# A list job that yields ahead of its TensorE steps, with look-ups asked in pairs and marked one ahead

## Chip, core and metric

The kernel runs on one core of a Trainium2 chip. The metric is the device time of one execution in microseconds, taken as the median of the runs shown.

## What is computed

One decoder layer over 256 tokens of width 2048: an attention part (a differential attention beside a sparse one), a norm, a retrieval part called PEER, and a second norm. The change lies in the retrieval part. Each token picks 8 x 16 of 16,384 experts by product keys, and the layer sums the picked rows of `v`, weighted by a gate and by the gelu of a product with the rows of `u`:

```
top_s, pos = lax.top_k(cand, PEER_TOPK)
eidx = jnp.take_along_axis(cidx, pos, axis=-1)
g = jax.nn.softmax(top_s, axis=-1)
ue = u[eidx]
h = jnp.einsum('cd,chkd->chk', xc, ue).astype(jnp.float32)
a = jax.nn.gelu(h, approximate=False) * g
ve = v[eidx]
return jnp.einsum('chk,chkd->cd', a.astype(ve.dtype), ve)
```

Not every expert is wanted by a token of the 256. So the kernel reads the first 32 groups of 128 experts whole, and of the other groups only the rows that somebody wants: it builds a list of wanted experts and gathers their rows by it. The list job is what the change rewrites.

## The kernel before

All engines run from one program order that is fixed while the program is built. Weight work comes in 273 units (`units`). A unit is 1 MB of weights: it is loaded (`dma_unit`, L165), split into a high part `wh` (ScalarE, ACT) and a low part `wl` (VectorE, DVE), and used in four quarters of matmuls on TensorE (PE). Units 77 to 108 are the whole groups of `u`. Units 109 to 162 (the C units) hold gathered rows of `u`: GpSimd (POOL) issues an indirect DMA from an index column, the rows are turned on PE (`turn_quarter`, L211, the rows `psa<-ident,raw`) one unit ahead, and then used. A quarter of a C unit is so one turn of 4 matmuls and 8 matmuls `psb<-xx`. C units 109 to 115 use tiles of 256 columns, the later ones up to unit 154 of 512. Units 163 to 272 are the value stage: rows of `v`, gathered and used without a turn.

A unit's weights are asked for three units ahead, and six units ahead in the value stage.

Beside the units run jobs, which are Python generators. After each quarter `run_units` (L268) calls `pump` (L235). It steps each job once, in the order in which they were started, up to the next `yield`. With a slack (2.5 us here, `SLACK_GATE`) it stops as soon as the builder's own estimate of the ACT or DVE clock is ahead of that of PE by more than the slack. A job that yields a positive number isn't stepped before that much estimated time is over. Three jobs matter:

- The list job (`job_list`, L1020). It makes a key for every group and position, sorts with 16 rounds of MAX8 and MATCH_REPLACE8 on DVE, finds the beginnings of the parts of the list with four small matmuls (`less`, `ones`, result `tot`) in the first round, turns the sorted keys into differences (`shift`, `edge`, copied into `dx`), and then makes 38 look-ups. One look-up marks on DVE (`sg`, one to three tiles), multiplies on PE (`psa<-dx,sg`, three matmuls for each mark tile), and reads the result on DVE (`at`, three times `lw`) and ACT (`i2l`). After look-ups 4, 9, 12, 17, 22, 28 and 38 `known` turns what was found into index columns (`vidx` for gathers of rows, `aidx` for gates).
- The gate job (`job_gates`, L1001), 32 steps for the second half of the tokens. A step makes one-hot tiles on DVE (two `oh` and one `og`), multiplies the tiles of two steps before on PE (`psa<-og,oh`, 8 matmuls) and copies out on ACT (`stg`). 32 more steps of the first half run earlier, in `job_count`.
- The singles (`job_singles`, L1280): 28 rows that one token alone wants, each with two gathers of 1 MB (`sr`), in four groups that begin with seven small gathers (`gsr`). They start at the unit at which the gate job has ended (`single_from`, L1554) and then follow the units' count, one for 1.5 C units.

Where a unit's gather needs an index column that the list hasn't reached, `column` (L179) pumps without slack until it is there: all jobs are stepped in turns, and no unit's matmul is put between. This comes three times: at unit 106 for the first 12 columns, at unit 118 for columns 27 to 35, and at unit 127 for columns 51 to 65. This text calls these places the first, second and third forced stretch.

## Time and profile before

| | us |
|---|---|
| median of 3 runs | 1737.91 (1737.27 to 1738.87) |
| profiled execution, device time | 1734.11 |
| its span, first to last instruction | 1732.2 |
| PE, share of the span busy | 93% |
| DVE, share of the span busy | 75% |

The profiled execution is 3.8 us (0.2%) below the median. PE is the engine that is nearly always at work, so the question for every stage is when it isn't, and what ended its wait. Note that the ends of matmuls are modelled: a stretch in which PE shows busy throughout may still run below PE's rate. PEclk is the clock granted to PE as a share of full speed; its two levels are 1.0 (2.4 GHz) and 0.5 (1.2 GHz), and a mean between them is a mixture.

### The profile page before, as it was taken

The numbers are of one execution on the slowest core, as the hardware profiler recorded it, in microseconds if no ns is written. First come the engines' busy times: TensorE is split into PE (matmuls) and PEld (weight loads), VectorE is DVE, ScalarE is ACT, GpSimd is POOL, SyncE is SP. The second block draws the span as 40 slices with busy tenths as digits, with TensorE's granted clock in tenths as the row PEclk, the third lists the DMA queues.
The fourth block names the chain that finished last, engine by engine and source line by source line (L and its number), as shares of the span: only waits on it lengthen the run. The fifth ranks groups of instructions, "written<-read, shape, count | busy, mean of one in ns | idle before, by whom it ended". The sixth has DMA issues, their size and how long they took to land.

```text
span 1732.2 us, 25235 instructions
## 1 busy us (share of the span) xinstructions
PE 1606.4 (93%) x9151; PEld 1364.4 (79%) x9151; DVE 1307.0 (75%) x2844; ACT 817.7 (47%) x1370; POOL 596.5 (34%) x558
## 2 busy tenths in 40 slices
PE   7999999998989899959979899999979999999994
PEld 6888888877878788849969788888857777788872
DVE  5686767656999887875976667786678888777767
ACT  5445555445424565323635333344445555555533
POOL 0033100015778400002001033334566666556742
PEclk9999999999989999979979899999999999999998
DMA  7454454545444434926324878798999999998861
GB/s 275 163 178 146 150 190 147 217 178 194 161 147 165 171 110 132 300 68 208 111 74 154 250 287 341 272 392 311 419 351 406 387 389 381 372 331 310 300 255 55
DMA packets 112531, 409.18 MB, mean 236 GB/s; under 512 B 11216, under 2 KB 62608, under 8 KB 69648
## 3 DMA queue, kind: packets, MB, share of 16 engines
q0 software_dynamic: 37856, 246.96, 37.4%
q1 hardware_dynamic: 74400, 160.27, 27.2%
q8 instruction: 74, 1.21, 0.3%
q14 instruction: 57, 0.47, 0.1%
q10 hardware_dynamic: 144, 0.26, 0.0%
HBM read 376.00 MB, written 31.39 MB: 235 GB/s over the span
## 4 chain that ended last, share of the span: by engine, by line
PE 64%; DVE 20%; DMA 6%; issue 4%; ACT 3%; POOL 2%; SPq 0%; DVEq 0%; ACTq 0%; POOLq 0%
PE psa L116 34%; PE psb L116 31%; DVE wl L116 6%; DVE oh L116 2%; ACT wh L116 2%; POOL gsr L187 1%; DMA gr<-gtab,aidx 1%; DMA sr<-x1d,xidx 1%; DVE lw L116 1%; DMA raw<-in_v_dram,vidx 1%; DVE tv L116 1%; DVE ti L116 1%; DVE yacc L116 1%; DVE eid L116 1%; DVE og L116 1%
## 5 line engine op out<-in xcount | busy, mean ns | idle before, releaser
L116 PE MATMUL psb<-xx,wh 128*128 128x512 f32 (+1 forms) x1407 | 504.8, 393 | 0.0
L116 DVE TENSOR_TENSOR wl<-raw,wh 128x1024 fp32r<-128x1024 f32 (+2 forms) x278 | 321.6, 1172 | 101.8 <-ACT wh L116 101.5
L116 PE MATMUL psb<-xx,wl 128*128 128x256 f32 x1392 | 373.6, 283 | 5.2 <-DVE wl L116 3.9
L116 ACT CAST wh<-raw 128x1024 fp32r<-128x1024 f32 (+1 forms) x278 | 283.5, 1044 | 65.4 <-PE psa L116 26.8
L116 PE MATMUL psa<-xx,wh 128*128 128x512 f32 x800 | 291.1, 407 | 9.4 <-DVE xx L116 8.3
L116 PEld LDWEIGHTS psb<-xx,wh 128*128 128x128 f32 x1407 | 268.3, 192 | 36.1
L116 PEld LDWEIGHTS psb<-xx,wl 128*128 128x128 f32 x1392 | 266.8, 192 | 11.3 <-DVE wl L116 5.4
L187 POOL DMA_INDIRECT raw<-in_un_dram,vidx x54 | 54.7, 1014 | 480.3 <-PE psa L116 252.1
L116 PE MATMUL psa<-xx,wl 128*128 128x256 f32 x800 | 219.2, 284 | 0.9 <-DVE wl L116 0.8
L116 DVE TENSOR_TENSOR wl<-psa,wh 128x512 fp32r<-128x512 f32 x216 | 146.6, 686 | 75.2 <-ACT wh L116 74.7
L116 ACT CAST wh<-psa 128x512 fp32r<-128x512 f32 x216 | 126.6, 587 | 149.9 <-PE psa L116 147.8
L116 PEld LDWEIGHTS psa<-xx,wh 128*128 128x128 f32 x800 | 151.0, 192 | 42.9 <-ACT wh L116 10.0
L116 PEld LDWEIGHTS psa<-xx,wl 128*128 128x128 f32 x800 | 153.9, 192 | 6.6 <-DVE wl L116 2.1
L116 DVE TENSOR_TENSOR wl<-rawv,wh 128x1024 fp32r<-128x1024 f32 x106 | 125.7, 1222 | 28.3 <-ACT wh L116 25.7
L116 PE MATMUL psa<-ident,raw 128*128 128x128 f32 x864 | 130.7, 274 | 3.4 <-DMA raw<-in_un_dram,vidx 3.4
L116 ACT CAST ah<-ar 128x256 fp32r<-128x256 f32 (+1 forms) x82 | 30.3, 370 | 201.3 <-DVE ar L116 192.3
L116 PE MATMUL psb<-wl,ah 128*128 128x512 f32 x276 | 110.2, 399 | 7.2 <-DVE wl L116 7.2
L116 PE MATMUL psb<-wh,ah 128*128 128x512 f32 x276 | 110.3, 400 | 3.4 <-DVE bl L116 2.6
L116 PEld LDWEIGHTS psa<-ident,raw 128*128 128x128 f32 x864 | 103.7, 142 | 11.8 <-issue 3.7
L116 PE MATMUL psa<-wh,ah 128*128 128x512 f32 x268 | 106.7, 398 | 4.9 <-ACT wh L116 4.9
L116 PE MATMUL psa<-wl,ah 128*128 128x512 f32 x268 | 107.7, 402 | 3.0 <-DVE wl L116 2.6
L116 PE MATMUL psb<-wh,al 128*128 128x512 f32 x276 | 109.1, 395 | 0.0
(305 smaller groups left out, 3050.7 us busy)
## 6 DMA issues: line engine op xcount, KB each, us to landing
raw<-in_win_dram SPq DMA_DIRECT2D x42, 1024.0 KB, 4.9
raw<-in_ut_dram SPq DMA_DIRECT2D x32, 1024.0 KB, 5.1
raw<-in_wo_dram SPq DMA_DIRECT2D x18, 1024.0 KB, 4.9
raw<-in_wq_dram SPq DMA_DIRECT2D x16, 1024.0 KB, 4.9
gtab<-stg SPq DMA_DIRECT2D x32, 512.0 KB, 5.4
cdr<-bl SPq DMA_DIRECT2D x39, 128.0 KB, 4.6
ar<-cdr SPq DMA_DIRECT2D x39, 128.0 KB, 7.1
hd<-bl SPq DMA_DIRECT2D x32, 128.0 KB, 1.7
```

Source lines behind the costliest of these rows:

```text
L116: return f(*a, **k)
L187: nc.gpsimd.indirect_dma_start(dst, None, src, bass.IndirectOffsetOnAxis(ap=index, axis=0))
```

## The change

Five edits, all in the list job:

- It yields before the four small matmuls for `tot`, and before the `shift` and `edge` matmuls.
- `begin` is one TENSOR_TENSOR of 304 elements in place of eight TENSOR_SCALAR of 38.
- ACT copies the first half of `dx` and DVE the second; before, ACT copied both large halves, and DVE the four small pieces.
- The first four look-ups are asked in pairs: marks of three look-ups first, then the matmuls of two look-ups, the fourth's marks, the matmuls of the next two, and the reads behind each pair's yield.
- From the fifth on, a look-up's marks are made right behind the read of the one before, and a look-up has two yields (the second asks for 2 us) in place of three.

```
@@ job_list
                 DVE.tensor_copy(t16, t8)
+                yield
                 ps = psA()
                 PE.matmul(ps[:, 0:8], less, c16, start=True, stop=False)
...
-                for c in range(8):
-                    DVE.tensor_scalar(begin[:, c], first, tot[:, c:c + 1], None, op0=OP.add)
+                DVE.tensor_tensor(begin, first[:, None].to_broadcast([P, 8, A]),
+                                  tot[:, 0:8, None].to_broadcast([P, 8, A]), op=OP.add)
...
         ACT.copy(XY[:, 0:P], srt)
+        yield
...
-        for h in range(2):
+        for h, copy in enumerate((ACT.copy, DVE.tensor_copy)):
             c, o = slice(4 * h, 4 * h + 4), h * m
-            ACT.copy(dx[:, c, 0:P], ps[:, None, o:o + P].to_broadcast([P, 4, P]))
...
+            copy(dx[:, c, 0:P], ps[:, None, o:o + P].to_broadcast([P, 4, P]))
...
-        for a, (part, q) in enumerate(ASK):
...
-                sg[c] = ls.tile([P, 3 * P], F16, name="sg", tag="sg", bufs=3)
-                DVE.tensor_scalar(sg[c], places, begin[:, c, a:a + 1], None, op0=OP.is_ge)
-            if a >= 4:
-                yield
...
+        def mark(a):
+            part, q = ASK[a]
+            marks[a] = {c: ls.tile([P, 3 * P], F16, name="sg", tag="sg", bufs=4)
+                        for c, at in start_of[part] if 3 * q + 2 >= at}
+            for c, sg in marks[a].items():
+                DVE.tensor_scalar(sg, places, begin[:, c, a:a + 1], None, op0=OP.is_ge)
...
+        for a in range(3):
+            mark(a)
+        yield
+        for a in (0, 2):
+            find(a)
+            find(a + 1)
+            if a == 0:
+                mark(3)
+            yield
+            read(a)
+            read(a + 1)
+        known(0, CUTS[0])
+        asked = CUTS[0]
+        mark(4)
+        yield 2000.0
+        for a in range(4, A):
+            find(a)
+            yield
+            read(a)
+            if a + 1 < A:
+                mark(a + 1)
             if 3 * (a + 1) in CUTS:
                 known(asked, 3 * (a + 1))
                 asked = 3 * (a + 1)
-            yield
+            yield 2000.0
```

`find(a)` holds the matmuls of look-up a, `read(a)` its `at`, `i2l` and `lw`.

Where the instructions come to stand follows from the jobs' turns. Three places:

DVE in the first forced stretch, from the copies into `dx` on. Before:

```order
L116 CAST dx<-psa 128x4 x4
L116 TENSOR_SCALAR sg<-places,begin 128x384
L116 SCALAR_TENSOR_TENSOR at<-psa,mine 128x3
L116 SCALAR_TENSOR_TENSOR lw,keys<-row,at,psa 128x128 x3
L116 TENSOR_SCALAR sg<-places,begin 128x384
```

After:

```order
L116 CAST dx<-psa 128x4x128
L116 CAST dx<-psa 128x4 x2
L116 TENSOR_SCALAR sg<-places,begin 128x384 x6
L116 SCALAR_TENSOR_TENSOR at<-psa,mine 128x3
L116 SCALAR_TENSOR_TENSOR lw,keys<-row,at,psa 128x128 x3
```

All six mark tiles of the first four look-ups stand ahead of the first read, where each look-up's marks stood behind the read of the one before. On PE the 18 matmuls of the four look-ups follow one another in both kernels, and then the same 64 matmuls of units 106 to 108 up to the first turn; the 8 matmuls of a quarter that stood between the `tot` and the `shift` matmuls now stand ahead of the `tot` matmuls.

DVE in the second forced stretch, from one look-up's read to the next one's (`oh`, `oh`, `og` are a gate step). Before:

```order
L116 SCALAR_TENSOR_TENSOR lw,keys<-row,at,psa 128x128 x3
L116 TENSOR_TENSOR oh_8700<-iota_3638,iT 128x512
L116 TENSOR_TENSOR oh_8701<-iotab,iT 128x512
L116 TENSOR_TENSOR og<-oh_8701,gpc 128x1024
L116 TENSOR_SCALAR sg<-places,begin 128x384 x2
L116 TENSOR_TENSOR oh_8720<-iota_3638,iT 128x512
L116 TENSOR_TENSOR oh_8721<-iotab,iT 128x512
L116 TENSOR_TENSOR og<-oh_8721,gpc 128x1024
L116 TENSOR_TENSOR oh_8743<-iota_3638,iT 128x512
L116 TENSOR_TENSOR oh_8744<-iotab,iT 128x512
L116 TENSOR_TENSOR og<-oh_8744,gpc 128x1024
L116 SCALAR_TENSOR_TENSOR at<-psa,mine 128x3
```

After:

```order
L116 SCALAR_TENSOR_TENSOR lw,keys<-row,at,psa 128x128 x3
L116 TENSOR_SCALAR sg<-places,begin 128x384 x2
L116 TENSOR_TENSOR oh_8617<-iota_3638,iT 128x512
L116 TENSOR_TENSOR oh_8618<-iotab,iT 128x512
L116 TENSOR_TENSOR og<-oh_8618,gpc 128x1024
L116 TENSOR_TENSOR oh_8640<-iota_3638,iT 128x512
L116 TENSOR_TENSOR oh_8641<-iotab,iT 128x512
L116 TENSOR_TENSOR og<-oh_8641,gpc 128x1024
L116 SCALAR_TENSOR_TENSOR at<-psa,mine 128x3
```

Two gate steps for a look-up in place of three, and the marks ahead of both. From the first turn to the end of the second forced stretch PE has 25 sets of 8 gate matmuls before and 18 after (with the same 40 quarters); from there to the end of the third 7 and 14 (with the same 36 quarters). In the third forced stretch PE has 30 look-up matmuls in a row before and 18 after; the other 12 stand in two quarters ahead of it.

POOL's queue at the passage into the value stage. Before, ahead of and behind the fourth group's seven small gathers:

```order
L187 DMA rawv<-in_v_dram,vidx 128x2048
L187 DMA gsr<-gtab,gi 128x128 x7
L187 DMA gr<-gtab,aidx 128x256
L187 DMA raw<-in_v_dram,vidx 128x2048
L187 DMA gr<-gtab,aidx 128x256
```

After, at the same place (a single's two gathers):

```order
L187 DMA raw<-in_v_dram,vidx 128x2048
L187 DMA sr<-in_un_dram,vidx 128x2048
L187 DMA sr<-x1d,xidx 128x2048
L187 DMA gr<-gtab,aidx 128x256
L187 DMA rawv<-in_v_dram,vidx 128x2048
```

The gate job ends four units later, so `single_from` is 135 in place of 131. 19 singles stand ahead of the first gather from `v` before, 16 after; the fourth group's seven gathers stand 15 issues of POOL behind that first gather from `v` before, 54 behind it after (rows of the same gather counted once), and the last single is done at unit 239 in place of 217.

## Rows read from the trace of the kernel before

**Rows 1.** The page: busy time of each engine, and the granted clock of PE in 40 equal slices of the span.

```profile
PE 1606.4 (93%) x9151; PEld 1364.4 (79%) x9151; DVE 1307.0 (75%) x2844; ACT 817.7 (47%) x1370; POOL 596.5 (34%) x558
...
PEclk9999999999989999979979899999999999999998
```

**Rows 2.** Busy time by stretches, cut at the places that the list touches. The columns: the stretch, its length, then busy us (and instructions) of PE, PEld, DVE, ACT and POOL, PEclk, the share of the DMA engines busy, GB/s.

```profile
748.60:789.60 41.00, 20.12 (x101) 16.39 (x101) 27.41 (x140) 6.02 (x15) 3.75 (x3) 0.71 0.17 55
...
816.50:868.40 51.90, 50.34 (x404) 47.57 (x403) 46.90 (x111) 30.25 (x51) 5.09 (x5) 1.00 0.34 117
868.40:890.80 22.40, 11.90 (x90) 9.61 (x90) 20.24 (x63) 8.56 (x12) 0.00 (x0) 0.58 0.00 1
890.80:966.00 75.20, 74.92 (x505) 67.55 (x504) 48.99 (x133) 37.01 (x69) 8.58 (x9) 0.99 0.56 187
966.00:978.50 12.50, 5.08 (x35) 3.56 (x36) 7.47 (x41) 0.81 (x5) 0.00 (x0) 0.71 1.03 279
978.50:1120.00 141.50, 136.26 (x923) 120.36 (x921) 97.81 (x267) 54.22 (x122) 45.30 (x48) 0.99 0.77 283
1120.00:1256.00 136.00, 129.03 (x925) 119.03 (x923) 99.69 (x198) 58.82 (x130) 57.78 (x57) 1.00 0.95 372
1256.00:1300.00 44.00, 34.88 (x134) 25.70 (x133) 31.56 (x45) 19.29 (x26) 29.98 (x27) 0.92 0.91 352
1300.00:1500.00 200.00, 198.59 (x846) 157.92 (x845) 164.03 (x210) 111.14 (x145) 129.64 (x106) 1.00 0.98 386
1500.00:1690.00 190.00, 187.04 (x800) 149.68 (x799) 140.41 (x190) 101.64 (x125) 111.18 (x102) 1.00 0.84 306
```

**Rows 3.** Who kept PE waiting from 740 to 1300 us: total us, times, longest us.

```profile
PE psa L116 <- DVE sg L116: 28.9, 15, 4.1
PE psa L116 <- DVE XX L116: 9.1, 1, 9.1
...
PE psa L116 <- DVE c L116: 4.1, 1, 4.1
```

**Rows 4.** PE's timeline in the first forced stretch: start, length, engine, line, operation, tiles, shapes, count, and in brackets the idle time before it and what ended it.

```profile
752.71 0.17 PE L116 MATMUL psa<-c,less 128*128 128x8 f16 x1 [4.13 <-DVE c L116]
...
764.91 1.25 PE L116 MATMUL psa<-XX,shift 128*128 128x137 f32 x4 [9.07 <-DVE XX L116]
...
768.68 0.51 PE L116 MATMUL psa<-dx,sg 128*128 128x130 f16 x3 [2.06 <-DVE sg L116]
...
777.00 0.78 PE L116 MATMUL psb<-xx,wh 128*128 128x512 f32 x1
```

**Rows 5.** Timelines of DVE, ACT and POOL in the same stretch, in order of time; the last row is a VectorE operation on 512 elements read from PSUM, from a later place.

```profile
753.82 1.28 DVE L116 TENSOR_SCALAR begin<-first,tot 128x38 f32<-128x38 f32 x8
...
764.47 0.29 DVE L116 MAX8 XX<-key 128x8 f32<-128x128 f32 x1
...
766.65 0.58 ACT L116 CAST dx<-psa 128x512 f16<-128x512 f32 x1 [1.56 <-PE psa L116]
...
769.22 0.16 DVE L116 SCALAR_TENSOR_TENSOR at<-psa,mine 128x3 f32<-128x3 f32 x1 [0.60 <-PE psa L116]
...
770.74 0.32 DVE L116 TENSOR_SCALAR sg<-places,begin 128x384 f16<-128x384 f16 x1
...
779.88 0.17 DVE L116 CAST vidx<-keys 128x12 int32<-128x12 f32 x1
...
781.07 1.20 POOL L187 DMA_INDIRECT raw<-in_un_dram,vidx  x1 [194.37 <-DMA hd<-bl]
...
845.11 0.69 DVE L116 TENSOR_TENSOR wl<-psa,wh 128x512 fp32r<-128x512 f32 x1 [0.75 <-ACT wh L116]
```

**Rows 6.** The view of DMA issues: a gather of C rows, how many, median us from issue to landing.

```profile
raw<-in_un_dram,vidx POOLq DMA_INDIRECT x54, 6.0
```

**Rows 7.** DVE's timeline in the second forced stretch: one gate step, one read, the next gate step, the marks.

```profile
875.46 0.68 DVE L116 TENSOR_TENSOR oh<-iota,iT 128x512 f16<-128x512 f16 x1
...
877.19 0.15 DVE L116 SCALAR_TENSOR_TENSOR at<-psa,mine 128x3 f32<-128x3 f32 x1
...
878.68 0.69 DVE L116 TENSOR_TENSOR oh<-iota,iT 128x512 f16<-128x512 f16 x1
...
880.41 0.54 DVE L116 TENSOR_SCALAR sg<-places,begin 128x384 f16<-128x384 f16 x2
```

**Rows 8.** PE's timeline: a set of gate matmuls and what follows it at full clock; the first look-up of the second forced stretch and the turn that ends the stretch; a look-up of the third forced stretch and the turn that ends it.

```profile
855.67 1.09 PE L116 MATMUL psa<-og,oh 128*128 128x128 f16 x8
856.51 0.48 PE L116 MATMUL psb<-xx,wh 128*128 128x512 f32 x1
...
873.64 0.95 PE L116 MATMUL psa<-dx,sg 128*128 128x130 f16 x6 [4.11 <-DVE sg L116]
...
890.81 1.04 PE L116 MATMUL psa<-ident,raw 128*128 128x128 f32 x4
...
968.54 0.69 PE L116 MATMUL psa<-dx,sg 128*128 128x130 f16 x6 [1.85 <-DVE sg L116]
...
977.44 1.06 PE L116 MATMUL psa<-ident,raw 128*128 128x128 f32 x4
```

**Rows 9.** POOL's timeline at the fourth group's small gathers, first and last of seven.

```profile
1271.56 1.68 POOL L187 DMA_INDIRECT gsr<-gtab,gi  x1 [4.07 <-DVE gi L116]
...
1279.95 0.94 POOL L187 DMA_INDIRECT gsr<-gtab,gi  x1 [0.31 <-issue]
```

More of the change, by code (lines that the diff above doesn't have):

```diff
@@ L1133, in job_list @@
         yield
-        for h in range(2):
+        for h, copy in enumerate((ACT.copy, DVE.tensor_copy)):
             c, o = slice(4 * h, 4 * h + 4), h * m
-            ACT.copy(dx[:, c, 0:P], ps[:, None, o:o + P].to_broadcast([P, 4, P]))
-            DVE.tensor_copy(dx[:, c, P:P + 1], ps[:, o + P + 4 * h:o + P + 4 * h + 4, None])
-            DVE.tensor_copy(dx[:, c, P + 1:P + 2], ps[:, None, o + P + 8:o + P + 9].to_broadcast([P, 4, 1]))
+            copy(dx[:, c, 0:P], ps[:, None, o:o + P].to_broadcast([P, 4, P]))
+            copy(dx[:, c, P:P + 1], ps[:, o + P + 4 * h:o + P + 4 * h + 4, None])
+            copy(dx[:, c, P + 1:P + 2], ps[:, None, o + P + 8:o + P + 9].to_broadcast([P, 4, 1]))
         keys, i2l = F([P, A, 3], "keys"), ls.tile([P, A, 3], F32, name="i2l", tag="XY")
@@ L1162, in known, with find, read @@
             keep["known"] = b
-        asked, start_of = 0, {"S0": ((0, 0),), "S1": ((1, 0),), "C": ((2, 0), (4, LC1), (5, LCS)),
-                              "D": ((3, 0), (6, LD1), (7, LDS))}
-        for a, (part, q) in enumerate(ASK):
-            cs = [c for c, at in start_of[part] if 3 * q + 2 >= at]
-            sg = {}
-            for c in cs:
-                sg[c] = ls.tile([P, 3 * P], F16, name="sg", tag="sg", bufs=3)
-                DVE.tensor_scalar(sg[c], places, begin[:, c, a:a + 1], None, op0=OP.is_ge)
-            if a >= 4:
-                yield
-            ps = psA()
+        start_of = {"S0": ((0, 0),), "S1": ((1, 0),), "C": ((2, 0), (4, LC1), (5, LCS)),
+                    "D": ((3, 0), (6, LD1), (7, LDS))}
+        marks, found = {}, {}
+        def mark(a):
[4 more added lines that the diff above has]
+                DVE.tensor_scalar(sg, places, begin[:, c, a:a + 1], None, op0=OP.is_ge)
+        def find(a):
+            ps, sgs = psA(), marks.pop(a)
+            cs = list(sgs)
             for j in range(3):
                 for c in cs:
-                    PE.matmul(ps[:, j * n:(j + 1) * n], sg[c][:, j * P:(j + 1) * P], dx[:, c],
+                    PE.matmul(ps[:, j * n:(j + 1) * n], sgs[c][:, j * P:(j + 1) * P], dx[:, c],
                               start=(c == cs[0]), stop=(c == cs[-1]))
-            pj = ps[:, 0:3 * n].rearrange("p (j x) -> p j x", j=3)
-            yield
+            found[a] = ps[:, 0:3 * n].rearrange("p (j x) -> p j x", j=3)
+        def read(a):
+            pj = found.pop(a)
             at = ls.tile([P, 3], F32, name="at", tag="at", bufs=2)
@@ L1190, in job_list @@
                 asked = 3 * (a + 1)
-            yield
+            yield 2000.0
         fl = F([P, 11], "fl")
```

## The prediction

> **What bounds the kernel now.** I read the page first: PE is busy 93% of the span, DVE 75%, and in the middle third of the slices the granted clock falls below full [rows 1]. So I looked for the stretches in which PE isn't fed, and cut the span there [rows 2]. From 748.6 to 789.6 us PE works 20 of 41 us; from 868.4 to 890.8 it works 12 of 22.4, at a mean clock of 0.58; from 966.0 to 978.5 it works 5 of 12.5. These are the three forced stretches. Two more are less plain: from 816.5 to 868.4 PE shows 50.3 of 51.9 us, but DVE too shows 46.9, so DVE nearly sets the pace there; and the passage into the value stage, 1256 to 1300, leaves PE idle for 9.1 us. The waits name the cause: 28.9 us in 15 waits for marks (`sg`), 9.1 for the end of the sort (`XX`), 4.1 for the first counts (`c`) [rows 3]. DVE works in order, so a wait for marks is a wait for everything that stands ahead of them on DVE: reads, and in the second forced stretch gate steps.
>
> From 1300 us on PE is busy 198.6 of 200 and 187.0 of 190 us [rows 2]. What is won before stays won, unless transfers are late.
>
> **First forced stretch.** The yields do not remove it: unit 106 still asks for columns that the list hasn't, so all jobs are pumped with no unit between. What moves is one quarter. Before, its 8 matmuls came after the `tot` matmuls; now they run ahead of them, at full clock and in time in which PE waited 4.13 us for `c` [rows 4]. The sort that ends with MAX8 at 764.76 [rows 5] holds PE in either kernel, so this moves no end. `begin` does: eight operations took 1.28 us from 753.82, on the chain of the sort. One of 304 elements lies between the 0.16 us of a tiny operation and the 0.69 of 512 elements [rows 5]; I take 0.5, so the sort ends 0.7 sooner, at 764.05. `shift` and `edge` follow as before, and the copies into `dx`, which began at 766.65, can begin at 765.95.
>
> Before, ACT's half took 0.58 and its second half waited for DVE's small pieces, so that the first look-up began at 768.68 [rows 4, 5]. Now both halves begin at 765.95. DVE's takes about 0.69 (its row of 512 elements from PSUM), two small copies 0.25, the first mark 0.3: the first look-up begins near 767.3, 1.4 sooner. The four look-ups are 18 matmuls. Three take 0.51 [rows 4], at the low clock, so 18 take 2.9; marks cost DVE 0.23 each behind the first and keep up. PE is through at 770.1. Before, each look-up also waited for the read of the one before (1.5 us from `at` at 769.22 to the next mark at 770.74 [rows 5]), and PE went on at 777.00 [rows 4]. That is 6.9 sooner. Of the 64 matmuls that follow (11 us in either kernel) the first came at half clock before; a little less of them will now, so the first turn could begin near 781.5 in place of 789.6.
>
> But the turn needs the first gather, and that needs the reads. They are still serial on DVE: six marks end near 768.6, four reads of 1.5 end at 774.7. Before, 3.05 us lay between 777.00 and the end of `vidx` at 780.05, of which 0.3 were the wait for the last matmuls and 1.5 the last read: 1.25 for `known`'s way to `vidx`, which so comes at 775.9. POOL issues 1.0 later as before, and the gather lands 6.0 after that [rows 5, 6]: 782.9. So PE waits about 1.3 us for it, a wait that wasn't there. **Gain 6.7 us** (41.0 becomes 34.3). Bounds: 4 if the gather takes 2.7 us more than the median, 8 if it doesn't hold PE.
>
> **Up to the second forced stretch** the list needs two turns of the jobs for a look-up instead of three, and fewer gate steps stand there: of 25 sets of gate matmuls up to the end of the second forced stretch 18 are left. 12 in place of 16 fall between 816.5 and 868.4. A gate step takes DVE 1.73 us (877.19 - 875.46 [rows 7]), so DVE loses 6.9 us; but one read (1.49), one mark and a `known` (about 1.6 with the operations behind `vidx`) come in from the forced stretch, net 3.6 less. PE loses four sets of 0.84 [rows 8], 3.4. With both engines near full, and gate steps now in some quarters only, I take **a gain of 2 us**; bounds 0 and 4.
>
> **Second forced stretch.** Between two look-ups DVE had two gate steps, a read, a gate step and the marks, 7.15 us for each (873.64 to 880.79 by PE). Now: a read and the marks, 1.95 us, then two gate steps, 3.46; and the first look-up's marks are made before the stretch. By DVE's order: gate, gate, read, marks (5.4), the same again (5.4), and the third look-up starts 10.8 us in; its six matmuls, 0.7 to 0.9, and two sets of gate matmuls, 1.7 at full clock, 2.2 taken, then the turn: 13.6 us against 22.4. **Gain 8.8 us**; bounds 5.2 (only the three gate steps fewer) and 10.5. A part of this, the 3.1 us of read and `known` counted above, is paid there.
>
> **Up to the third forced stretch** the gate steps come back: 14 sets in place of 7 in the same 36 quarters. PE is the bound here (74.9 of 75.2 us, DVE 49.0 [rows 2]), so each costs its matmuls, 0.84 us: 5.9 us. Two look-ups that were in the third forced stretch stand here too, 12 matmuls, 0.7 us at full clock. DVE has 26 us free and gets 12.1 + 3.5 of them filled; where a gate step and a read fall into one quarter it has 0.7 + 1.7 + 1.7 to do against PE's 1.9 + 0.84 (75.2 us less seven sets, by 36 quarters), and sets the pace there, for which I add 1.4. **Loss 8 us**; bounds 6.6 and 13 (seven steps at DVE's 1.73, and the finds).
>
> **Third forced stretch.** A look-up's marks still follow the read of the one before, so a run of look-ups still waits 1.85 us in each [rows 8]. But there are three in place of five: two times 1.85 + 0.69 less, so that the 11.4 us from the stretch's start at 966.0 to the turn at 977.44 [rows 2, 8] become 6.3. With the low clock behind it (0.71 in the stretch's row) in part kept off, **gain 6 us**; bounds 4 and 7.
>
> **Later look-ups.** Between 978.5 and 1120 PE is idle for 5.2 us [rows 2], most of it for marks. With marks made a turn ahead I take **a gain of 3**; bounds 0 and 5, since DVE also stands behind the singles' small gathers there, which nothing removes.
>
> **Passage into the value stage.** From 1120 to 1300 PE is idle 7.0 + 9.1 = 16.1 us [rows 2]. In the passage POOL waits 4.07 us and issues seven small gathers from 1271.56 to 1280.9 [rows 9]: for 14 us no row of `v` is asked for, with three units asked ahead. That group now comes some 40 issues later, where six units are asked ahead, and this stall should go; but three singles more, 6.3 MB, fall into a stage in which the DMA engines are 0.91 to 0.98 busy at 386 GB/s [rows 2], and the third group comes nearer to the passage. 6.3 MB are 16 us of transfer at that rate if nothing hides them. I take **a gain of 2** and bounds of 9 gained and 8 lost.
>
> **Sum:** 6.7 + 2 + 8.8 - 8 + 6 + 3 + 2 = 20.5 us off the profiled execution's 1734.1, 1713.6; that execution is 3.8 below the median, so in terms of the median 1737.9 - 20.5 = **1717.4**.
>
> **Rivals.**
> - *The gate steps come back at DVE's price.* If DVE and not the list sets the pace from 816 to 966, moving steps wins little: nothing ahead of the second forced stretch, 5.2 in it, a loss of 10 after it, 6.7 and 4 in the other two, 1 later, 1 in the passage. 7.9 us, 1730. For it: DVE's 46.9 of 51.9. Against: DVE's 49.0 of 75.2 where the steps go [rows 2].
> - *The passage loses its stall.* With the fourth group out of it and nothing given back: 9 in place of 2, and 1 or 2 more in the earlier terms, 29 us, 1709.
> - *Transfers bind the value stage.* Then the 6.3 MB cost 16 us, and the fourth group's block of 14 us on POOL costs its whole length, since in a stage bound by transfers every us without a request is lost; singles at the same pace up to unit 239 leave no slack to make it good. Of the gain 20.5 - 2 are left, minus 30: 1749, slower. It decides if the share of busy DMA stays near 1 until the last single. For it: 0.98 from 1300 to 1500. Against: 0.84 from 1500 on, 30 us of free transfer time, and PE's 198.6 of 200 [rows 2]. The Trainium skill, "DMA: Bandwidth & Descriptors", section "Where 436 GB/s comes from", says that a core's transfers between HBM and SBUF are held to about 358 GB/s; by that rule this rival would be the forecast. The trace does not agree: it moves 386 GB/s for 200 us.
> - *The change does nothing*, since every wait is in forced stretches and these remain: each term at its low bound, 3 + 0 + 5.2 - 13 + 4 + 0 + 0, about zero: 1738.
>
> **How the numbers follow.** The forecast 0.58, its own span 1712 to 1724; the first rival 0.18, the second 0.13, the third 0.06, the last 0.05. A measurement of this kernel can tell about 0.2%, 3.5 us, from no change. Faster: 0.58 + 0.18 + 0.13 = 0.89; within 0.2%: 0.05; slower: 0.06. The range leaves out the last two and the far ends of the others: 1705 to 1732.
>
> **What would show it.** In the changed profile: a look-up run of 18 matmuls without waits near 767 us; one wait of PE for a gather, 1 to 2 us, near 782; a second forced stretch of 13 to 15 us; the stretch from its end to the next forced one longer by 7 to 9, with DVE near 64 us busy; no wait above 1 us for marks after that. Wrong would be: waits for `og` in place of those for `sg`, or waits for `raw` or `rawv` gathers behind 1300.

## The result

| | us |
|---|---|
| before, median of 5 runs | 1738.87 (1737.27 to 1742.22) |
| changed, median of 5 runs | 1726.66 (1724.44 to 1729.97) |
| ratio, 95% interval | 0.9925 (0.9908 to 0.9943) |
| profiled execution of the changed kernel; its span | 1727.36; 1725.2 |

The change makes the kernel faster by 0.75%, 12 to 13 us. The forecast was 1717.4, with 1705 to 1732 as the range: the range held, the forecast's own span (1712 to 1724) missed by 2.7, and of the 20.5 us forecast some 12 came.

**The profile after, by stretches.** The first view is busy time cut where [rows 2] were cut, at the corresponding places, in the same columns:

```profile
751.30:784.50 33.20, 16.98 (x93) 14.70 (x92) 25.87 (x129) 5.00 (x15) 3.93 (x3) 0.69 0.13 45
...
860.60:873.50 12.90, 6.80 (x53) 5.51 (x53) 11.64 (x34) 3.95 (x6) 0.00 (x0) 0.60 0.00 0
873.50:956.60 83.10, 83.07 (x579) 75.62 (x577) 62.87 (x172) 44.07 (x78) 9.07 (x9) 0.98 0.47 158
956.60:961.80 5.20, 1.53 (x12) 1.01 (x13) 3.37 (x18) 0.32 (x2) 0.00 (x0) 0.71 0.92 247
961.80:1103.70 141.90, 139.03 (x965) 125.02 (x963) 98.88 (x299) 54.25 (x127) 38.52 (x39) 0.99 0.79 285
...
1232.00:1280.00 48.00, 39.52 (x164) 31.53 (x165) 33.69 (x45) 23.46 (x34) 27.16 (x24) 0.93 0.92 365
1280.00:1480.00 200.00, 194.27 (x809) 152.72 (x808) 160.43 (x208) 105.94 (x136) 128.83 (x110) 0.98 0.96 377
```

The first forced stretch has gone from 41.0 to 33.2 us (1.4 of that is the quarter that now stands ahead of it), the second from 22.4 to 12.9, the third from 12.5 to 5.2, and the stretch between the second and the third has grown from 75.2 to 83.1, with PE busy throughout: the gate steps are there now. The last row is the surprise. PE did 846 matmuls in the first 200 us behind the passage [rows 2]; now it does 809, with 5.7 us idle.

Who kept PE waiting from 740 to 1300 us (us, times, longest), to be held against [rows 3]:

```profile
PE psa L116 <- DVE sg L116: 11.2, 6, 2.4
PE psa L116 <- DVE XX L116: 11.0, 1, 11.0
...
PE psa L116 <- DVE c L116: 2.7, 1, 2.7
```

28.9 us of waits for marks became 11.2, and 15 waits became 6. The wait for the sort grew by 1.9 us and the one for `c` shrank by 1.4: the quarter that was moved ahead of the `tot` matmuls no longer fills the wait behind them.

**Where the time went, aligned.** Executions differ in their first 730 us too, where the programs are the same. So for each kernel the table takes the start of the same PE matmul in its trace, less that in the trace of the kernel before, less the same difference at a matmul that starts at 730.46 us before (1.3 us for the changed kernel, -0.6 to 3.3 for the others). The row names are its start in the kernel before. Negative is sooner. The columns behind "after" are the experiments below, by their numbers.

```
   before  after    e1    e2    e3    e4    e5    e6    e7    e8    e9   e10   e11   e12
   789.58   -6.4   0.2  -5.2  -6.3  -6.2  -0.5  -6.3  -5.4  -6.2  -5.6  -6.3  -5.5  -5.6  first turn
   864.03   -9.0  -0.3  -7.9  -8.9  -8.8  -3.1  -7.3  -8.7  -8.8  -7.3  -8.9  -8.7  -7.3  last turn ahead of stretch 2
   890.81  -18.6   0.1 -17.4 -18.5 -18.4 -12.7  -5.3 -25.6 -18.4 -24.3 -18.5 -25.8 -24.1  turn that ends stretch 2
   963.78  -10.8   0.7 -10.3 -10.8 -11.2  -5.5  -6.7 -11.1 -10.6  -9.8 -11.3 -11.1  -9.7  last turn ahead of stretch 3
   977.44  -16.9   1.0 -16.4 -16.9 -17.4 -11.6  -3.6 -20.6 -16.8 -19.3 -17.5 -20.6 -19.2  turn that ends stretch 3
  1117.19  -18.1   3.0 -15.7 -16.7 -18.5 -13.1  -9.9 -23.1 -17.0 -21.7 -19.3 -23.7 -21.9  behind the look-ups
  1221.23  -21.4   4.4 -20.5 -13.5 -21.9 -17.9  -8.9 -25.5 -18.5 -21.4 -21.4 -30.7 -28.8  ahead of the passage
  1303.93  -18.5   5.0 -17.2 -12.6 -18.5 -15.3  -4.7 -17.7 -18.4 -18.6 -29.8 -36.6 -29.3  value stage, first use of ah + 96
  1407.40   -8.9   5.0  -8.0  -4.8 -16.5  -6.2  -0.8 -16.4 -14.1 -14.8 -28.0 -32.9 -25.5  first use of ah + 352
  1708.15   -8.1   4.8  -6.1  -5.1 -14.6  -6.1  -1.8 -13.0 -14.6 -14.9 -21.5 -28.0 -21.2  first use of ah + 1080
```

Up to 1304 us the changed kernel is 18.5 us ahead. By 1407 it is 8.9 ahead: **9.6 us are lost in the value stage**, where the prediction had nothing. The loss shows again in the columns of e2 (9.2) and e5 (9.1), which have the fourth group at the same place, and not in that of e1, which has it where it was. (The profiled execution of before, 1734.11, is 4.8 below the median of its 5 runs, that of e1 3.6 above its own. So the end of a column says less than the medians; a column against its neighbours, stretch by stretch, says more. The last row is one of the last matmuls; what follows it is not in the table.)

**The place of the loss.** POOL's timeline of the changed kernel:

```profile
1330.40 1.93 POOL L187 DMA_INDIRECT rawv<-in_v_dram,vidx  x1 [1.98 <-DVE one L116]
1336.47 1.68 POOL L187 DMA_INDIRECT gsr<-gtab,gi  x1 [4.14 <-DVE gi L116]
...
1345.31 0.95 POOL L187 DMA_INDIRECT gsr<-gtab,gi  x1 [0.30 <-DMA gsr<-gtab,gi]
1346.56 1.02 POOL L187 DMA_INDIRECT raw<-in_v_dram,vidx  x1 [0.30 <-issue]
1347.88 0.94 POOL L187 DMA_INDIRECT gr<-gtab,aidx  x1 [0.30 <-issue]
```

The fourth group's seven small gathers first wait 4.14 us for their index `gi`, then take ten, and from 1332.3 to 1346.6 no row of `v` and no row of gates is asked for. DVE and PE behind that, each from its own timeline:

```profile
1352.90 0.43 DVE L116 TENSOR_TENSOR ar<-ar,gr 128x256 f32<-128x256 f32 x1 [4.95 <-DMA gr<-gtab,aidx]
```

```profile
1354.77 0.80 PE L116 MATMUL psa<-wh,ah 128*128 128x512 f32 x1 [2.36 <-ACT ah L116]
```

The gate row asked for at 1347.88 is the one that DVE waits for, and `ah` is made from it. The stretches around it, in ten-microsecond pieces:

```profile
1340.00:1350.00 10.00, 10.00 (x45) 8.04 (x44) 6.96 (x9) 4.40 (x5) 7.87 (x8) 1.00 0.36 101
1350.00:1360.00 10.00, 7.18 (x21) 5.05 (x20) 5.97 (x9) 4.39 (x5) 7.09 (x7) 0.74 1.01 393
1360.00:1370.00 10.00, 9.89 (x40) 7.64 (x39) 7.97 (x11) 4.50 (x6) 6.83 (x6) 0.92 0.93 345
1370.00:1380.00 10.00, 8.95 (x37) 6.44 (x36) 9.00 (x11) 4.40 (x5) 6.72 (x5) 1.00 1.01 410
```

The DMA engines fall to a busy share of 0.36, and then PE starves: 21, 40 and 37 matmuls in pieces that hold 44 at full pace, 34 too few, which at 10/44 us each are 7.7 of the 9.6 us. Only 4 us of that are idle time (30 less the three busy times); the rest is PE at a granted clock of 0.74 and 0.92 behind the wait.

**The passage itself** is hardly better. With the fourth group gone from it, PE still idles 8.5 of the 48 us from 1232 to 1280, where it idled 9.1 of 44 before. Its longest wait is 3.97 us, up to 1268.22, and the longest piece of the chain of waits up to it (start, length, what) is this:

```profile
1252.97 13.36 DMA gr<-gtab,aidx
```

A row of gates took 13.4 us from issue to landing there, with no small gather near it.

### The profile page after: what moved, and what is told of

Same layout as the page of the kernel before. It is cut to its first block, busy times and chain, and to the rows that moved or that the text cites. A ratio compares the mean times of both kernels' runs of the same rounds, so it can differ in the third digit from the quotient of the medians.

```text
span 1725.2 us, 25232 instructions
## 1 busy us (share of the span) xinstructions
PE 1609.9 (93%) x9151; PEld 1371.0 (79%) x9151; DVE 1304.4 (76%) x2836; ACT 815.2 (47%) x1371; POOL 598.2 (35%) x558
## 4 chain that ended last, share of the span: by engine, by line
PE 65%; DVE 18%; DMA 5%; issue 5%; ACT 3%; POOL 3%; SPq 0%; DVEq 0%; ACTq 0%; POOLq 0%
PE psa L116 33%; PE psb L116 32%; DVE wl L116 6%; ACT wh L116 2%; DVE oh L116 2%; DMA gr<-gtab,aidx 2%; POOL gsr L187 1%; DMA raw<-in_win_dram 1%; DVE tv L116 1%; DVE ti L116 1%; DVE yacc L116 1%; DVE eid L116 1%; DVE lw L116 1%; DMA rawv<-in_v_dram,vidx 1%; DVE cand L116 1%
## 5 line engine op out<-in xcount | busy, mean ns | idle before, releaser
L187 POOL DMA_INDIRECT gr<-gtab,aidx x82 | 96.2, 1174 | 40.5 <-issue 22.2
```

The lines of the kernel that those rows point to most:

```text
L187: nc.gpsimd.indirect_dma_start(dst, None, src, bass.IndirectOffsetOnAxis(ap=index, axis=0))
```

## Experiments

The theories are named in the expectations. A is the prediction's account of the time up to 1300 us, with the loss behind it put down to the fourth group's block on POOL. B puts losses down to transfers (more singles in the value stage). C, D and E are rivals on single points. Medians are of runs beside the kernel before on the same chip.

| | median | ratio to before, 95% |
|---|---|---|
| e1 front edits alone | 1738.46 | 0.9998 (0.9987 to 1.0009) |
| e2 loop alone | 1730.33 | 0.9950 (0.9934 to 0.9967) |
| e3 singles counted from 131 | 1728.84 | 0.9940 (0.9925 to 0.9956) |
| e4 fourth group ahead | 1718.83 | 0.9881 (0.9864 to 0.9898) |
| e5 no pairs | 1731.28 | 0.9958 (0.9944 to 0.9972) |
| e6 three turns for a look-up | 1735.79 | 0.9987 (0.9978 to 0.9996) |
| e7 = e4, list job alone in forced stretches | 1724.98 | 0.9925 (0.9911 to 0.9940) |
| e8 = e4, second and third group ahead too | 1718.95 | 0.9891 (0.9872 to 0.9910) |
| e9 = e8 with e7's edit | 1720.61 | 0.9887 (0.9869 to 0.9905) |
| e10 = e8, slower singles | 1715.48 | 0.9861 (0.9842 to 0.9880) |
| e11 = e9, slower singles | 1716.45 | 0.9882 (0.9866 to 0.9899) |
| e12 = e9, pace between | 1718.00 | 0.9880 (0.9862 to 0.9897) |

**e1: the edits ahead of the look-ups alone.** The kernel before with the two yields, the one `begin`, and the shared `dx` copies; the look-ups' loop as it was. The last of them, on the kernel before:

```
-        for h in range(2):
+        for h, copy in enumerate((ACT.copy, DVE.tensor_copy)):
             c, o = slice(4 * h, 4 * h + 4), h * m
-            ACT.copy(dx[:, c, 0:P], ps[:, None, o:o + P].to_broadcast([P, 4, P]))
+            copy(dx[:, c, 0:P], ps[:, None, o:o + P].to_broadcast([P, 4, P]))
```

> Only the edits ahead of the look-ups (two yields, begin in one operation, the copies into dx shared by ACT and DVE); the look-ups as before. Theory A (the terms as forecast, and the time lost again near 1336 to 1380 us by the fourth group's seven small gathers): the first forced stretch is about 2 us shorter (0.7 from begin, 1.4 from dx), the rest as in the kernel before, with the singles where they were: 1737, ratio 0.998 to 1.000. Theory B (the extra 6.3 MB of singles in the value stage cost the time): the same here, 1737. Theory C (the edits ahead of the look-ups carry the gain, and the loop gives back what it wins): 1727 to 1730, ratio near 0.994.

1738.46, no difference from before. The first look-up does come 0.95 us sooner, but the first turn does not (0.2 later in the table). From the last of the four look-ups to the first turn, before and then e1, in two views by stretches:

```profile
776.29:789.60 13.31, 13.31 (x71) 11.62 (x72) 7.60 (x25) 3.52 (x7) 3.75 (x3) 0.86 0.51 168
```

```profile
778.60:793.10 14.50, 14.47 (x71) 12.57 (x72) 7.62 (x25) 3.52 (x7) 3.76 (x3) 0.78 0.53 190
```

The same 71 matmuls take 1.2 us more, at a granted clock of 0.78 in place of 0.86: what was won up to the first look-up is given back through the clock in this trace. That this comes of the longer idle time ahead (11.05 us in one piece for the sort, 9.07 before [rows 4]) is not shown; the traces in the last section speak against it. The 2 us expected counted `begin` twice: the prediction's 1.4 held it. By the table's reckoning the `shift` matmuls begin 0.8 us sooner, so that `begin` brought what was forecast (0.7) and the shared copies 0.15 in place of 0.7. Theory C falls.

**e2: the loop alone.** The kernel before with the new loop, and so all of the change but the edits of e1:

```
-        for a, (part, q) in enumerate(ASK):
...
+        for a in (0, 2):
+            find(a)
+            find(a + 1)
...
+        for a in range(4, A):
+            find(a)
```

> Only the look-ups' loop (pairs, marks one ahead, two yields); what stands ahead of it as before. Theory A: the changed kernel less the 2 us of the front edits: 1729, ratio 0.993 to 0.995, with the second forced stretch at 13 us and a loss of some 9 us behind 1336 us where the fourth group's gathers stand. Theory B: the same time, the loss spread over the value stage. Theory C: 1737 or more.

1730.33, within 1.4 us of what A said; the loss behind 1304 us is there too (-17.2 to -8.0). Of the 6.4 us of the first stretch the loop alone brings 5.2. With the pairs in place the front edits are worth the remaining 1.2 there. By the medians they are worth 3.7 us on top of the loop; but the intervals of the two kernels overlap, so it isn't settled that they are worth more than the 1.2.

**e3: the singles counted from where they were.**

```
-    single_from = pos["k"]
+    single_from = 131
```

> The changed kernel with the singles' turns counted from unit 131 as they were, not from 135; the job starts at 135 all the same. The fourth group's small gathers then come some 16 units earlier, at the start of the value stage, and two more singles lie ahead of the value stage. Theory A: the stall of about 14 us on POOL stays and only moves towards the passage: within 3 us of the changed kernel, 1724 to 1730. Theory B: 4.2 of the 6.3 MB leave the value stage, 11 us at 386 GB/s: 1716 to 1720.

1728.84, no better than the changed kernel: A. The singles' bytes go back ahead of the value stage and nothing is won. The block is only elsewhere (POOL's timeline, first and last small gather and the next row):

```profile
1283.23 1.68 POOL L187 DMA_INDIRECT gsr<-gtab,gi  x1 [6.41 <-DVE gi L116]
...
1292.02 0.94 POOL L187 DMA_INDIRECT gsr<-gtab,gi  x1 [0.30 <-issue]
1293.27 0.95 POOL L187 DMA_INDIRECT gr<-gtab,aidx  x1 [0.31 <-issue]
```

6.41 us of waiting for `gi`, then ten of gathers. In the table e3 loses 4.1 us between 1117 and 1304, and 7.8 more up to 1407, right behind the block:

```profile
1300.00:1310.00 10.00, 6.81 (x22) 4.67 (x21) 8.91 (x12) 4.39 (x5) 8.16 (x7) 0.83 1.01 398
```

That is the picture of the changed kernel's 1350 to 1360 us, 50 us sooner. Behind 1407 nothing is lost.

**e4: the fourth group's gathers ahead.** A job of its own asks for the fourth group (`AHEAD` is 3 alone) from unit 159 on, one small gather for each quarter, and makes its sums there. `group` holds the lines that stood in the singles' job:

```
+    def job_groups():
+        for g in AHEAD:
+            while pos["k"] < single_turn((g - 1) * SGRP + 2):
+                yield
+            yield from group(g * SGRP, True)
...
         for r in range(SGRP):
+            if spread:
+                yield
             gather(gr[:, r], gtab.rearrange("e (t s) -> (e t) s", t=2), gi[:, r:r + 1])
```

> The changed kernel, with the fourth group's seven small gathers asked one for each quarter from unit 159 on, its sums made there too, and the singles themselves where the changed kernel has them (to within some units). The same bytes move. Theory A: POOL is nowhere closed for 14 us in the value stage, and the loss near 1350 us goes: 1716 to 1719, ratio near 0.988. Theory B: no change, 1725 to 1728. A third outcome, 1721 to 1724, would say that the spread gathers cost some of it again in the passage.

1718.83: A, in its middle, and clear of the changed kernel (the intervals don't touch). The loss from 1304 to 1407 us is 2.0 in place of 9.6. POOL now has rows between the small gathers:

```profile
1218.37 0.95 POOL L187 DMA_INDIRECT gsr<-gtab,gi  x1 [3.70 <-DVE gi L116]
1220.82 0.94 POOL L187 DMA_INDIRECT raw<-in_v_dram,vidx  x1 [1.50 <-PE psa L116]
...
1229.26 0.96 POOL L187 DMA_INDIRECT gsr<-gtab,gi  x1 [0.30 <-issue]
1230.52 1.05 POOL L187 DMA_INDIRECT gr<-gtab,aidx  x1 [0.30 <-issue]
```

The first 200 us behind 1280 do 837 matmuls in place of 809:

```profile
1280.00:1480.00 200.00, 197.22 (x837) 156.48 (x838) 164.69 (x212) 112.30 (x144) 128.38 (x108) 1.00 1.00 393
```

By POOL's order the edit moves six singles (the 16th to the 21st) one to seven units later as well, so it isn't the block alone that differs; but the DMA engines are busier here (1.00 against 0.96) and PE is faster, which speaks against B.

**e5: no pairs.** The changed kernel with the first four look-ups in the same loop as the others:

```
-        for a in range(3):
-            mark(a)
...
-        for a in range(4, A):
+        asked = 0
+        mark(0)
+        yield
+        for a in range(A):
             find(a)
```

> The changed kernel with the first four look-ups asked one by one, each marked behind the read of the one before, as the later ones are; all else the same, the later order too. Theory A (in the first forced stretch the gain comes from the pairs, since a run of look-ups otherwise waits for read and marks in each): three waits of 1.85 us for marks come back near 772 us, the stretch is 39 to 41 us long as in the kernel before, 6 us above the changed kernel: 1732 to 1734. Theory D (making a look-up's marks right behind the read of the one before is enough, and pairing adds nothing): 1726 to 1728.

1731.28, a little under A's 1732 to 1734. The three waits are back (PE's timeline):

```profile
771.71 0.51 PE L116 MATMUL psa<-dx,sg 128*128 128x130 f16 x3 [1.93 <-DVE sg L116]
774.07 0.95 PE L116 MATMUL psa<-dx,sg 128*128 128x130 f16 x6 [1.86 <-DVE sg L116]
776.87 0.95 PE L116 MATMUL psa<-dx,sg 128*128 128x130 f16 x6 [1.85 <-DVE sg L116]
```

The table's first column entry falls from -6.4 to -0.5. Marks made right behind the read of the look-up before don't shorten a run of look-ups; asking four before reading any does. D falls.

**e6: three turns for a look-up.**

```
             yield 2000.0
+            yield
```

> The changed kernel with one yield more for each look-up from the fifth on, so that the list needs three turns of the jobs for a look-up as before; marks stay one ahead. Theory A (what shortens the second and third forced stretch is the list's pace against the gate steps, two turns for three): the second forced stretch is 20 to 23 us again, the third 10 to 13, the gate job ends at unit 130; the gain of the first stretch alone is left: 1731 to 1734. Theory D (marks one ahead are what counts): 1725 to 1729.

1735.79, 2 us worse than A's range, and far from D. The second forced stretch comes out longer than before by 2.0 (864.03 to 890.81 in the table), the third by 3.1, with, by the program's order, 12 sets of gate matmuls in the second (11 before, 7 changed) and 33 look-up matmuls in the third (30 and 18): with the 2 us of waiting on top of three turns the list is slower than it was. The list's pace against the gate steps decides, as the prediction had it.

**e7: the list job alone in the forced stretches.** On e4, `column` steps nothing but the list:

```
         while keep.get("known", 0) <= c:
-            pump()
+            pump(only="job_list")
```

> The kernel with the fourth group's gathers ahead (1718.8), and in the forced stretches the list job alone is stepped: no gate step and no single between look-ups. The second forced stretch then has one set of gate matmuls in place of seven, the third one look-up in place of three; six gate steps go to the quarters behind. Theory A (a gate step that goes into quarters of full PE work costs its matmuls there, 0.84 us): the second stretch 5.5 to 7 us in place of 12.9, the third about 1.5 in place of 5.2, 5 us given back: 1712 to 1715. Theory E (it costs DVE's 1.73 us wherever it stands): 10.4 us given back, 1717 to 1720.

1724.98, which no theory gave. The stretches are as A has them: the second is 7.3 us shorter than in e4, the third 3.3. Behind the second, 14.5 us are given back against 7.2, so that all of its 7.3 us are gone by 964. Of the 7.3 more, 0.7 are 12 look-up matmuls, so the six gate steps cost 1.1 each, between their matmuls (0.84, A) and DVE's 1.73 (E), nearer to A. Then 25.5 us ahead at 1221 become 17.7 at 1304. DVE's timeline:

```profile
1258.82 1.08 DVE L116 TENSOR_REDUCE gate<-gsr 128x7 f32<-128x896 f32 x1 [9.98 <-DMA gr<-gtab,aidx]
```

The gate job ends two units later there, so the fourth group's sums fall into the passage. They wait 10 us, with `one` and all of DVE's queue behind them. The profile names a row of gates as what ended the wait; the sums read the small gathers, the last of which was asked for at 1250.00, behind a single's two gathers of 1 MB and rows of `v`. PE's longest wait from 1240 to 1270 us:

```profile
PE psa L116 <- DVE one L116: 9.6, 1, 9.6
```

**e8: the second and third group ahead too** (`AHEAD` is 1, 2 and 3), and the fourth done at unit 155.

```
-            while pos["k"] < single_turn((g - 1) * SGRP + 2):
+            while pos["k"] < single_from + 6 * g:
```

> The kernel with the fourth group's gathers ahead (1718.8), and now the second and third group's too, one small gather for each quarter, the groups six units apart from unit 141 on, so that the fourth group's sums are made at unit 155 and not in the passage. Theory A (every block of seven small gathers, and the 4 us of DVE sums behind it, costs PE a wait wherever rows are asked for just in time): the waits near 1205 to 1210 us (3.7 us) and the one of 5.2 us for bl near 1245 go: 1710 to 1714. Theory B (those waits are late rows of a stage bound by transfers, and another will take their place): 1717 to 1720.

1718.95, as e4: A's further gain isn't there, and B's words are what came: the waits moved. The two longest waits of PE from 1200 to 1300 us, and, from the chain of waits, the step from which that of 3.4 us follows (start, length, what):

```profile
PE psa L116 <- ACT wh L116: 5.1, 1, 5.1
PE psb L116 <- ACT wh L116: 3.4, 1, 3.4
```

```profile
1214.52 14.16 DMA raw<-in_v_dram,vidx
```

A row of `v` takes 14.2 us from issue to landing, where a gather of C rows took 6.0 [rows 6]. This wait is a late transfer. e8 doesn't move the groups alone, though: 17 singles stand ahead of the first gather from `v`, 15 in e4, and so 4.2 MB more come ahead of the passage.

**e9, e10, e11, e12: is the passage bound by transfers?** e9 puts e7's edit on e8. e10 slows the singles of e8 to one for 2.25 C units, e11 those of e9; e12 is e11 with a pace of 1.85 between.

```
-        k = single_from + 1.5 * i
+        k = single_from + 2.25 * i
```

> The list job alone stepped in the forced stretches (1725.0 with the fourth group at unit 165) and the second to fourth group's small gathers ahead, the fourth done at unit 158. Up to 1220 us the trace should stand 25 us before that of the kernel before, as with the list alone. Theory A (the passage costs what a group's block and sums cost): the wait of 9.6 us at 1253 us goes, 1710 to 1714. Theory B (the passage is bound by transfers, so that whoever comes there sooner waits longer): 1717 to 1722.

> The kernel with the second to fourth group ahead (1719.0), one single for 2.25 C units in place of 1.5: 11 singles in place of 16 are done by unit 162, so some 10 MB leave the stretch up to the passage and go behind 1300 us, where each single has more time until it is needed. Theory B (rows that took 14 us from issue to landing near 1215 us are late because transfers fill the DMA engines): the waits of 3.5 and 5.1 us in the passage shrink, 1710 to 1715. Theory A (they are POOL's and DVE's queues): 1717 to 1720. A third outcome, above 1722, would be the singles that come too late for their units at the end, or 10 MB too many behind 1300.

> Both: the list job alone in the forced stretches, the groups ahead, one single for 2.25 C units. Theory B: what the list alone wins ahead of the passage (7 us) is kept, since the transfers no longer bind there: 1704 to 1710. Theory A: as with both without the slower singles, within 2 us of that run.

> The same as the last run (list alone, groups ahead), with one single for 1.85 C units, between 1.5 and 2.25: the last single is then done at unit 251 and the one before it at 245, in place of both within the last few units ahead of their use, and 12 singles are done by unit 162. Theory B: the 33 us that it stood ahead of the kernel before until 1590 us are kept to within 3 us on both sides, since the last singles come in time: 1709 to 1714. If the passage needs the slower pace, a wait comes back there and the time is 1715 to 1719.

e9, 1720.61, lies in B's range. It is 21.7 us ahead behind the look-ups, 4.7 more than e8, and 18.6 at 1304 us, as e8 is (18.4). But its trace doesn't show B's cause. PE's longest wait there is 9.3 us, up to 1218, and it stands behind DVE, which waits for the fourth group's sums as in e7. The group's last small gather on POOL, and the sum on DVE:

```profile
1205.04 0.95 POOL L187 DMA_INDIRECT gsr<-gtab,gi  x1 [0.30 <-issue]
```

```profile
1213.90 1.09 DVE L116 TENSOR_REDUCE gate<-gsr 128x7 f32<-128x896 f32 x1 [9.12 <-issue]
```

The profile names nothing that ended DVE's wait; the sum reads what that gather brings, and begins 8.9 us after it was asked for, behind a single's two gathers of 1 MB. e7's wait of 9.6 us at 1253 has moved with its group. So A's cause is at work too, through DVE's queue and not through POOL's.

e10, 1715.48: B, half a microsecond above its range. The same view as for e8, the longest waits by their length:

```profile
PE psb L116 <- DVE bl L116: 1.6, 1, 1.6
PE psa L116 <- ACT wh L116: 1.5, 2, 1.3
```

The waits of 5.1 and 3.4 us are gone, and at 1304 us e10 is 29.8 ahead against e8's 18.4. From 1200 to 1300 us, e8 and then e10, in the columns of [rows 2]:

```profile
1200.00:1300.00 100.00, 87.65 (x469) 74.11 (x469) 70.18 (x98) 45.05 (x76) 56.20 (x47) 0.93 0.97 382
```

```profile
1200.00:1300.00 100.00, 94.14 (x505) 78.49 (x504) 74.99 (x105) 50.15 (x81) 58.68 (x51) 0.98 1.01 400
```

The DMA engines are no less busy in e10. What has changed is what they carry: fewer of the singles' rows, which are wanted later, stand ahead of the rows that PE waits for (11 singles ahead of the first gather from `v`, 17 in e8). That is read from one trace of each; the medians don't settle it, since the intervals of e8 and e10 overlap.

e11 keeps what the list alone wins (36.6 at 1304), and DVE's wait for the fourth group's sums is 1.1 us there. By the table e10 and e11 give 6.5 and 4.9 us back behind 1407, most of it behind 1590: the last singles come just in time for their units. PE's waits in e11 from 1570 to 1690 us, the largest sum of them:

```profile
PE psb L116 <- DVE wl L116: 5.5, 8, 0.8
```

And behind the last matmul e11 loses 6.4 us more, which the table doesn't have: 26.4 us lie there, 20.0 before. The second norm is made in two halves. In the kernel before, the first begins at 1685.77, between the last units; in e11 both begin behind the last matmul, which ends at 1684.0 (DVE's timeline):

```profile
1687.48 0.24 DVE L116 BATCH_NORM_AGGREGATE mv<-bst 128x2 f32<-128x24 f32 x1
...
1694.55 0.25 DVE L116 BATCH_NORM_AGGREGATE mv<-bst 128x2 f32<-128x24 f32 x1
```

Why the first half was put off there was not tried. e11's median, 1716.45, is above B's 1704 to 1710, and 4.2 below e9's, which A didn't have either; its profiled execution, 1712.36, is the fastest of its runs (the slowest took 1721.05), so its column flatters it. e12 was to have both ends and has neither: a wait of 5.9 us near 1202 us is back, again behind the fourth group's sums, and 4.3 us still go behind 1407. 1718.00.

```profile
1203.42 1.09 DVE L116 TENSOR_REDUCE gate<-gsr 128x7 f32<-128x896 f32 x1 [5.80 <-DMA gsr<-gtab,gi]
```

e4 and e8 to e12 all have lower ratios than the changed kernel (e8's interval just touches its); among them the intervals overlap. e10 has the lowest ratio, 0.9861.

## Why the prediction was right or wrong

By its own terms (from the table, for the profiled execution):

| term | forecast | measured |
|---|---|---|
| first forced stretch | -6.7 | -6.4 |
| up to the second | -2 | -2.6 |
| second forced stretch | -8.8 | -9.6 |
| up to the third | +8 | +7.8 |
| third forced stretch | -6 | -6.1 |
| later look-ups, to 1117 | -3 | -1.2 |
| passage, to 1304 | -2 | -0.4 |
| value stage, behind 1304 | 0 | +10.4 |
| sum | -20.5 | -8.1 |

**The step that failed** is the sentence "What is won before stays won, unless transfers are late", and with it the passage's "this stall should go". The prediction saw that the fourth group would move from the passage to some 40 issues later. It took six units asked ahead for enough cover, so it counted the stall as gone. It wasn't: 14.2 us without a request outlasted what had been asked for. Nor did the passage lose its idle time when the group left it (8.5 us in place of 9.1): a late row of gates stands there, so the group's block was not all that the passage waits for. The gate row was late first, not a row of `v`, and of the 9.6 us lost there 7.7 are counted above. The third rival had the mechanism ("the fourth group's block of 14 us on POOL costs its whole length") but tied it to 16 us of transfer for 6.3 MB. These were not paid: e3 has 19 singles ahead of the first gather from `v` again and wins nothing, e4 has 15 and wins 7.8. That the range held is in part luck: the 10.4 us of the value stage were in no term of the sum, and the range was wide enough for them because it took in the first rival's 1730.

**The forced stretches came out as worked out,** each within 0.8 us. The 18 look-up matmuls stand in one run, 2.1 us long where 2.9 was reckoned, and the first turn waits for its gather, 0.59 us in place of 1.3 (PE's timeline of the changed kernel):

```profile
768.98 2.13 PE L116 MATMUL psa<-dx,sg 128*128 128x130 f16 x18 [1.91 <-DVE sg L116]
...
784.49 0.63 PE L116 MATMUL psa<-ident,raw 128*128 128x128 f32 x4 [0.59 <-DMA raw<-in_un_dram,vidx]
```

e5 shows that the pairs carry this stretch, e6 that the pace of two turns carries the second and third. The second's 9.6 us are worth little by themselves: 7.8 of them go again up to the third, as the prediction had it.

**The gate steps' price** was the first rival's question. Its time, 1730, is nearer to the measured 1726.7 than the forecast of 1717.4 is, but that is luck: by the stretches it is wrong, with nothing won ahead of the second forced stretch (measured 2.6), 5.2 in it (9.6) and 10 lost behind it (7.8). Seven steps and two look-ups cost 7.8 where the forecast had 8, and e7's six steps cost 1.1 each. The last rival's sum took 3 for the first stretch where the prediction's own bound was 4, and no loss in the passage where the bound was 8; nothing hangs on it.

**The terms of the edits in front** were right in their sum and wrong in one step. The two halves of `dx` don't begin together (below), which put the first look-up 0.4 later than worked out; alone these edits bring nothing that the medians show (e1).

**Later look-ups** were over-sized: no wait for marks above 1 us is left behind the third stretch, as forecast, but only 1.2 us came of it. What took the rest was not tried.

**Still open:** the profiled pair differs by 6.8 us and the medians by 12. Where the other executions of the kernel before lose what its profiled one didn't, no trace here shows; e1's trace, with the list's and the gate steps' order as before, loses 3.7 us between 964 and 1221 us and so gives one place.

## What to carry to other kernels

When a change moves work in program order, follow each queue to the end of the program. A block of small gathers that moves closes its queue for its whole length wherever it lands: 14.2 us closed cost 9.6 here. Asking one for each quarter took most of that away (e4), but the operation that reads the gathers must then stand late enough: where the last of them is queued behind rows of 1 MB, the reader holds up all of its engine's queue (e7, e9, e12).

A run of look-ups that waits for read and marks in each is shortened by asking several before reading any (e5). Stepping nothing else between them shortens it too, but what was left out is paid in the stretch behind: the second forced stretch of e7 gave all of its 7.3 us back.

Time won in one stage isn't kept by itself. e9 and e11 differ in one number, the singles' pace, and stand 18 us apart at 1304 us in their traces. Their medians differ by 4 us and their ratios to before by 0.0005: what the slower pace wins in the passage comes due at the last singles and in the second norm.

## What the runs showed of the hardware

ACT and DVE copy different columns of one PSUM tile into different halves of `dx`. ACT's timeline and DVE's of the changed kernel:

```profile
767.11 0.73 ACT L116 CAST dx<-psa 128x512 f16<-128x512 f32 x3 [1.56 <-PE psa L116]
```

```profile
767.87 0.84 DVE L116 CAST dx<-psa 128x512 f16<-128x512 f32 x3 [2.66 <-ACT dx L116]
```

DVE begins 0.03 us after ACT has ended and was released by it, so in this program the two engines don't share this read. That both write `dx` needn't be the reason. In a look-up's read, in the kernel before, ACT waits for DVE's `at` and then DVE for ACT's `i2l`, and these have nothing in common but the PSUM tile that they read:

```profile
769.50 0.16 ACT L116 COPY i2l<-psa 128x3 f32<-128x3 f32 x1 [1.36 <-DVE at L116]
769.69 0.35 DVE L116 SCALAR_TENSOR_TENSOR lw<-row,at,psa 128x128 f32<-128x128 f32 x1 [0.30 <-ACT i2l L116]
```

The Trainium skill, "PSUM — Partial Sum Buffer", section "PSUM bank collisions raise a hardware error", says that the compiler back end's scheduler adds a dependency between any two instructions of different engines on the same bank and quadrant, reads included. The trace agrees.

The clock cost time beyond the waits: behind the 2.4 us wait at 1352 us PE ran at 0.74. How much it costs differs from trace to trace, and the idle time ahead doesn't say it. Behind the look-ups, the same 64 matmuls of units 106 to 108 in e1 and in e12, each with 11.05 us of idle time for the sort ahead of the look-ups (the views count three more that overlap the ends):

```profile
779.34:793.08 13.74, 13.74 (x67) 11.96 (x65) 7.43 (x24) 3.52 (x7) 3.76 (x3) 0.80 0.56 199
```

```profile
772.76:784.87 12.11, 12.11 (x67) 10.37 (x64) 8.91 (x42) 3.75 (x9) 3.78 (x3) 0.93 0.20 57
```

Before, with 9.07 us of idle time, they took 12.6; in e2, with 9.08, 13.3. The first turn doesn't follow the clock where the look-ups stand in pairs: it waits for its gather, 0.4 to 0.6 us where the 64 matmuls took 13.0 to 13.3 (1.3 and 1.5 in e11 and e7), and 1.5 to 2.3 where they took 12.1 to 12.2.

With this core alone the DMA engines moved up to 410 GB/s in ten microseconds (1370 to 1380 above) and 393 for 200 us (e4). The Trainium skill, "HBM Reference", section "Specifications (TRN2)", says in its table and the note under it that a core that streams alone measures near 425 GB/s, above its share of 358. The trace agrees with that rather than with the limit that the prediction quoted.
